# First mixing stage: attention's outputs wait in the place of its queries, and keys and values are projected early

## The chip, the cores and the metric

The kernel runs on one core of one Trainium2 chip. The metric is the device time of one execution in microseconds (us); a version's time is the median of several executions. One execution of each version is also recorded by the hardware profiler, and every duration below comes from such a record.

## The reference, cut to what matters

The program is two blocks one after the other on 256 tokens of width 1024. The first block has two layers, and each layer works on 256 latent tokens and 256 context tokens. The change is in the mixing part of the layers, above all of layer 0, where both kinds of tokens get an output:

```
hl = rms_norm(xl, norm_mix) * (1.0 + sc1_l) + sh1_l        # latents; hc is the same for the context
aq_l, ak_l, av_l, mq_l, mk_l, mv_l, mo_l, mg_l, pp_l = jnp.split(hl @ w_in, IN_OFFSETS, -1)
att_l = block_attention(q_l, jnp.concatenate([k_l, k_c], 1), jnp.concatenate([v_l, v_c], 1))
hm_c, hm_l = bidir_mlstm(...)              # a gated recurrence in two directions, 4 heads
ml_l = mlstm_readout(hm_l, mo_l, ml_norm)
pool_l = pool_mix(pp_l, pool_w, pool_scale)
xl = xl + g1_l * (jnp.concatenate([att_l, ml_l, pool_l], -1) @ w_out)
...
if with_ctx_out:                           # layer 0 only
    att_c = block_attention(q_c, k_c, v_c)
    ml_c, pool_c = ...
    xc = xc + g1_c * (jnp.concatenate([att_c, ml_c, pool_c], -1) @ w_out)
```

The factors sc, sh and g of both layers come from a further product, `silu(c) @ w_ada + b_ada`, whose matrix has 1024 x 6144 elements in each layer. After the mixing comes a gated feed-forward part in each layer. The second block (feed-forward, a mixer with a scan, feed-forward) isn't touched by the change.

## The kernel before

Values are kept transposed: 128 features on the partitions, tokens along the free axis, the 256 context tokens first and the 256 latents behind them. Each float32 product with a large weight is made of three matmuls (`mm3`, lines 235 to 237): weight and input are each split into a high part in a faster format and a low rest, on ScalarE (line 228 for weights, 256 for inputs) and VectorE (229 and 257). A column of 128 outputs of such a product (`dense`) loads its weights by SyncE's queue (line 219, function `raw`) into one of four buffers `wr`, splits them into `wh` (3 buffers) and `wl` (2 buffers), and multiplies. In layer 0 a column of the projection `w_in` has 8 x 3 matmuls of 512 tokens.

The projection of layer 0 has 17 columns. Each has a name: `a0` to `a3` are attention's queries, `ak` and `av` its keys and values, `k0 k1 q0 q1 v0 v1 g o0 o1` belong to the recurrence (mLSTM), and `p0 p1` to pooling. Their order is the string `order` in `MIX[0]`. The first three are computed before the stage proper, together with the norm that feeds them.

The rest of the stage is written as Python generators, which issue instructions until they `yield`. `_mix` lets them take turns. In each round every generator takes as many steps as its number in `MIX` says:

```
def _mix(*gens):
    live = [(iter(g), n) for g, n in gens]
    while live:
        for item in list(live):
            for _ in range(item[1]):
                if next(item[0], item) is item:
```

- `projections` issues one column a step, and marks it as there in the set `got` when it takes the next step.
- `mlstm` takes 25 steps (one for the gates, and for each of four heads four score tiles and two directions) and then three for its outputs. Its gates go through a small DRAM buffer `Md` (lines 872 and 891) on the same queue as the weights.
- `attention` takes one step for the split of the keys and then ten for each of the four query columns `a{j}`: four tiles of 128 queries by one head for the latents and one for their product with the values, then the same for the context. A tile is: scores on TensorE (line 788), maximum on VectorE, exponential on ScalarE, scaling on GpSimd (798), transposes on TensorE (801), a copy on ScalarE (802). The product with the values is line 807, into the PSUM tile `p3`, of which there is one.
- `pool_mix` (`fill`) takes four steps. Each is a chain of five or seven operations on GpSimd (lines 823 to 831), a matmul (834) and a split.
- `late` is the second half of the output product: 8 columns with the weights of rows 512 to 1023 of `w_out`, and it starts when mLSTM and pooling have given all their outputs.
- `ada` computes the factors, 26 steps in this stage: 16 for layer 0 and 10 that layer 1 needs only later. A step loads two blocks of 512 KB of `w_ada` into the same buffers `wr` and multiplies from them directly (line 374, 16 recorded matmuls a step), then a copy (383), two transposes (386) and two small operations on VectorE (388, 389). All of it goes through the one PSUM tile `p2`, which mLSTM's products (939) and the transposes of the values (479) use as well.

A waiting generator (`after`) yields without issuing anything. The framework then lays down a fixed order of instructions for each engine, in which the earlier issued goes first where both can run, and adds the semaphores. So instructions of one round can stand among those of its neighbours, but the loads on SyncE's queue stand in the order in which the rounds issue them, apart from loads that wait for data.

The outputs of attention, mLSTM and pooling go into `mixh` and `mixl`. In layer 0 these take the memory of the normed input `xh` and `xl`, which all projections read. So `free` in layer 0 is `after(*order)`: nothing may be written there until all 17 columns have been issued. Attention meets this wait right behind its first product with the values:

```
yield from free()
self.split(mixh[:, j, q0:q0 + 256], mixl[:, j, q0:q0 + 256], po)
```

When the generators are done, `resid_norm` computes the first half of the output product from attention's outputs (weights rows 0 to 511 of `w_out`, 16 loads of 256 KB), first for the context and then for the latents, together with the norm of the feed-forward part.

Layer 1 uses the same functions with `MIX[1]`. It has outputs for the latents alone, its `mixh` and `mixl` have memory of their own, and so `free` waits for nothing there.

Of the kernel before, what the change touches and what calls it, by code (L numbers as in the profile page):

```python
# [10 lines left out]
AF = mybir.ActivationFunctionType  # L11
# [9 lines left out]
    "natural_log": (AF.Ln,),  # L21
}
NOSYNC = mybir.DependencyInfo(mybir.DependencyClass.NoSync, mybir.DependencyReason.SCHED_ONLY)
MIX = {0: {'order': 'k0 g q0 v1 v0 a2 k1 q1 av a1 a0 a3 ak o0 p0 o1 p1', 'ada_own': 16, 'ada_next': 10, 'proj': 2, 'ml': 5, 'att': 1, 'fill': 1, 'late': 3, 'ada': 1, 'split': 0, 'split2': 1}, 1: {'order': 'ak k0 g a0 v0 q0 a1 av k1 q1 v1 a2 a3 p0 o0 o1 p1', 'ada_own': 10, 'ada_next': 0, 'proj': 3, 'ml': 9, 'att': 2, 'fill': 1, 'late': 1, 'ada': 1}, 2: {'in': 4, 'att': 2, 'solve': 1, 'att2': 5, 'gate': 1, 'even': 1, 'odd': 1, 'fill': 9, 'early': 5}, 'ada_ffn': [0, 0], 'norm0': 2, 'norm1': 2}
NEG = -1.0e30
EPS = 1e-6
GN_EPS = 64e-5
# [96 lines left out]
# [7 lines that stand above are left out]
                    live.remove(item)  # L131
                    break
        yield
# [18 lines left out]
def _run(g):  # L152
    for _ in g:
        pass


class Builder:
# [281 lines left out]
    def layer(self, l, pre, beside, done):  # L439

        nc, a, tc = self.nc, self.a, self.tc
        x, mod = self.x, self.mod[l]
        both = l == 0
        T0 = 0 if both else 256
# [3 lines left out]
        with ExitStack() as es:  # L448
# [9 lines left out]
            ak = ap.tile([128, 512], F32, name="ak")  # L458
# [128 lines left out]
            def projections():  # L587
                for i, p in enumerate(order[n0:], n0):
                    c, every, use = proj[p]
                    yield from self.dense(w, (c,), full if every else part, use, T=512 if every else T,  # L590
                                          halves=l and i < 2)
                    got.add(p)
                    if both and i == n0:
                        self.late_consts()
# [8 lines left out]
            mix = lambda k, c0, c1: (mixh[:, k, c0 - T0:c1 - T0], mixl[:, k, c0 - T0:c1 - T0])  # L603
            with tc.tile_pool(name=f"ml{l}", bufs=1, reuse_waits="tile") as mp:
                ml = _chain(self.mlstm(l, mp, gz, mq, mk, mvt, mo, mixh, mixl, T0, after, free), mark("ml"))
                att = self.attention(l, mp, aq, rq, nq, ak, avt, mixh, mixl, T0, after, free)
                fill = _chain(after("p0", "p1"), free(), self.pool_mix(l, pp, mixh, mixl, T0), mark("pool"))
                late = _chain(after("ml", "pool"), self.resid(a["w_out"][l], mix, ((4, 8),), T0, 512, m(2, 1), m(2, 0)))
                ada = _chain(self.ada(l, n["ada_own"], at=(2,)), self.ada(1, n["ada_next"], at=(2,)))
                _run(_mix((projections(), n["proj"]), (ml, n["ml"]), (att, n["att"]), (fill, n["fill"]),  # L610
                          (late, n["late"]), (ada, n["ada"])))
            if both:
                xn = self.room("xn", [128, 2, 8, 512], F32R)
# [139 lines left out]
        nc.gpsimd.tensor_mul(lat, lat, c1["cos"])  # L753
        nc.vector.tensor_add(lat, lat, rs)

    def attention(self, l, ap, aq, rq, nq, ak, avt, mixh, mixl, T0, after, free):
        nc = self.nc
        yield from after("ak")

        kk = ap.tile([128, 2, 2, 512], F32R, name="kk")  # L760
        half = lambda e: slice(64 * e, 64 * e + 64)
        for kv in range(2):
            for e in range(2):
                nc.scalar.activation(kk[half(e), kv, 0], ak[half(kv)], AF.Copy)
            for e in range(2):
                nc.vector.tensor_sub(kk[half(e), kv, 1], ak[half(kv)], kk[half(kv), kv, 0].bitcast(F32))
        yield
        streams = [(256 - T0, 4)] + ([(0, 2)] if T0 == 0 else [])
        for j in range(4):
            yield from after(f"a{j}")  # L770
            for q0, nk in streams:
                kv = j // 2
                qq = ap.tile([128, 2, 256], F32R, name="qq", bufs=2)
                for e in range(2):
                    src = aq[half(e), j, q0:q0 + 256]
                    nc.scalar.activation(qq[half(e), e], src, AF.Copy)
                    nc.vector.tensor_sub(qq[half(1 - e), e], src, qq[half(e), e].bitcast(F32))
                po = self.ps(3, [128, 256])
                pts = []
                for e in range(2):  # L780
                    pt = ap.tile([128, 4, 256], F32, name="pt", bufs=2)
                    pts.append(pt)
                    for qt in range(2):
                        ps = self.ps(1, [128, 512])
                        s = ps[:, 0:128 * nk]
                        c = (q0 + 128 * qt) // 128
                        for i in range(2):
                            nc.tensor.matmul(s, qq[:, e, 128 * qt:128 * qt + 128], kk[:, kv, i, 0:128 * nk],  # L788
                                             start=i == 0, stop=i == 1)
                        st = ap.tile([128, 4], F32, name="st", bufs=8)  # L790
                        nc.vector.reduce_max(st[:, 0:1], s, axis=AX.X)
                        nc.vector.tensor_mul(st[:, 1:2], st[:, 0:1], nq[:, c, 2 * j + e:2 * j + e + 1])
                        pr = ap.tile([128, 512], F32, name="pr", bufs=2)
                        p = pr[:, 0:128 * nk]
                        self.fn(p, s, AF.Exp, bias=st[:, 1:2], scale=rq[:, c, 2 * j + e:2 * j + e + 1],
                                accum_out=st[:, 2:3])
                        nc.vector.reciprocal(st[:, 3:4], st[:, 2:3])
                        nc.gpsimd.tensor_scalar(p, p, st[:, 3:4], 0.0, op0=OP.mult, op1=OP.add)
                        pp = self.ps(0, [128, 4, 128])
                        for kt in range(nk):  # L800
                            nc.tensor.transpose(pp[:, kt, :], p[:, 128 * kt:128 * kt + 128], self.ident)
                        nc.scalar.activation(pt[:, 0:nk, 128 * qt:128 * qt + 128], pp[:, 0:nk, :], AF.Copy)
                        yield
                yield from after("av")
                for kt in range(nk):
                    for e in range(2):
                        nc.tensor.matmul(po[64 * e:64 * e + 64, :], avt[:, kt, 64 * kv:64 * kv + 64], pts[e][:, kt, :],  # L807
                                         start=kt == 0, stop=kt == nk - 1)
                yield from free()
                self.split(mixh[:, j, q0:q0 + 256], mixl[:, j, q0:q0 + 256], po)  # L810
                yield

    def pool_mix(self, l, pp, mixh, mixl, T0):
        nc, c1 = self.nc, self.c1
# [841 lines left out]
```

## Time and profile before

| what | value |
|---|---|
| time of the runs shown | 1891.31 us median of 3 (1889.07 to 1895.42) |
| profiled execution | 1892.11 us, of which the recorded span is 1890.3 us |
| granted TensorE clock over the span | 0.985 of full speed |
| layer 0's mixing stage, from its fourth column to the last product of attention | 54.8 to 294.5 us of the span |
| first matmul of `resid_norm` behind it | 298.41 us |

The span runs from the first to the last recorded instruction; 1.8 us of the profiled execution lie around it. "Busy" of an engine is the time in which at least one of its instructions was running. Ends of matmuls are modelled, and a matmul overlaps with the next, so short pauses between small matmuls don't show as idle time. PEld is the loading of TensorE's weights, which overlaps with its matmuls.

### The profile page before, as it was taken

The numbers are of one execution on the slowest core, as the hardware profiler recorded it, in microseconds if no ns is written. First come the engines' busy times: TensorE is split into PE (matmuls) and PEld (weight loads), VectorE is DVE, ScalarE is ACT, GpSimd is POOL, SyncE is SP. The second block draws the span as 40 slices with busy tenths as digits, with TensorE's granted clock in tenths as the row PEclk, the third lists the DMA queues.
The fourth block names the chain that finished last, engine by engine and source line by source line (L and its number), as shares of the span: only waits on it lengthen the run. The fifth ranks groups of instructions, "written<-read, shape, count | busy, mean of one in ns | idle before, by whom it ended". The sixth has DMA issues, their size and how long they took to land.

```text
span 1890.3 us, 34101 instructions
## 1 busy us (share of the span) xinstructions
PE 1821.8 (96%) x13552; PEld 1602.4 (85%) x13552; DVE 1115.2 (59%) x2130; ACT 920.4 (49%) x1662; POOL 260.6 (14%) x357
## 2 busy tenths in 40 slices
PE   7999999999999999999999999998999999899998
PEld 4677567888888897878999999998989987799998
DVE  5566656433333365886676565568778854466554
ACT  4544467322222355666555544446755543354443
POOL 1011423000000021232000110023654010010000
PEclk8998999999999999999999999999999999999999
DMA  9443667332333365445667666665544430166664
GB/s 309 125 117 90 188 203 232 114 101 73 106 101 89 93 184 155 124 146 179 181 185 203 191 172 181 187 190 163 158 126 131 123 101 7 34 177 180 180 183 129
DMA packets 490607, 279.26 MB, mean 148 GB/s; under 512 B 18240, under 2 KB 487240, under 8 KB 490320
## 3 DMA queue, kind: packets, MB, share of 16 engines
q1 hardware_dynamic: 490016, 275.33, 50.0%
q8 instruction: 106, 1.74, 0.4%
q10 hardware_dynamic: 432, 1.75, 0.3%
q14 instruction: 53, 0.43, 0.1%
HBM read 274.93 MB, written 2.12 MB: 147 GB/s over the span
## 4 chain that ended last, share of the span: by engine, by line
PE 84%; DVE 6%; DMA 4%; issue 3%; ACT 2%; POOL 1%; SPq 0%; POOLq 0%; ACTq 0%; DVEq 0%
PE pd L235 17%; PE pd L237 17%; PE pd L236 17%; PE p L235 6%; PE p L236 6%; PE p L237 6%; PE p L374 2%; DMA wr<-in_w_in_dram 1%; DVE wl L229 1%; PE p L807 1%; PE p L788 1%; ACT wh L228 1%; PE p L1496 1%; DMA wr<-in_w_ada_dram 1%; DMA wr<-in_w_out_dram 1%
## 5 line engine op out<-in xcount | busy, mean ns | idle before, releaser
L228 ACT ACTIVATE wh<-wr 128x1024 fp32r<-128x1024 f32 (+4 forms) x450 | 436.9, 972 | 621.2 <-PE pd L236 297.5
L229 DVE TENSOR_TENSOR wl<-wr,wh 128x1024 fp32r<-128x1024 f32 (+4 forms) x450 | 510.4, 1135 | 181.6 <-PE pd L237 102.6
L235 PE MATMUL pd<-xh,wh 128*128 128x256 f32 (+1 forms) x1168 | 362.7, 312 | 13.7 <-ACT wh L228 7.8
L237 PE MATMUL pd<-xh,wl 128*128 128x256 f32 (+1 forms) x1168 | 357.7, 307 | 1.6 <-DVE wl L229 1.4
L235 PEld LDWEIGHTS pd<-xh,wh 128*128 128x128 f32 x1168 | 224.5, 193 | 32.1 <-ACT wh L228 9.3
L237 PEld LDWEIGHTS pd<-xh,wl 128*128 128x128 f32 x1168 | 224.6, 192 | 15.7 <-DVE wl L229 6.0
L235 PE MATMUL pd<-hh,wh 128*128 128x256 f32 (+1 forms) x781 | 228.2, 294 | 0.0
L236 PE MATMUL pd<-hl,wh 128*128 128x256 f32 (+1 forms) x781 | 227.3, 293 | 0.0
L236 PE MATMUL pd<-xh,wh 128*128 128x256 f32 x792 | 225.8, 285 | 0.0
L237 PE MATMUL pd<-hh,wl 128*128 128x256 f32 (+1 forms) x781 | 223.5, 294 | 0.2 <-DVE wl L229 0.2
L314 POOL TENSOR_TENSOR ssa<-ssa,sq 128x256 f32<-128x256 f32 x54 | 47.6, 882 | 805.0 <-ACT sq L312 536.2
L236 PEld LDWEIGHTS pd<-xh,wh 128*128 128x128 f32 x792 | 152.3, 192 | 1.9 <-issue 1.3
L235 PEld LDWEIGHTS pd<-hh,wh 128*128 128x128 f32 x781 | 146.8, 188 | 4.7
L236 PEld LDWEIGHTS pd<-hl,wh 128*128 128x128 f32 x781 | 146.7, 188 | 4.6
L237 PEld LDWEIGHTS pd<-hh,wl 128*128 128x128 f32 x781 | 144.8, 188 | 4.9 <-DVE wl L229 0.4
L236 PE MATMUL pd<-xl,wh 128*128 128x512 f32 (+1 forms) x376 | 132.1, 353 | 0.2 <-DVE xl L359 0.2
L732 DVE TENSOR_TENSOR sg<-sg,p 128x256 f32<-128x256 f32 (+1 forms) x66 | 33.6, 510 | 158.3 <-PE p L237 158.0
L235 PE MATMUL p<-xh,wh 128*128 128x256 f32 (+1 forms) x360 | 103.1, 286 | 0.0
L237 PE MATMUL p<-xh,wl 128*128 128x256 f32 x352 | 99.8, 283 | 0.0
L236 PE MATMUL p<-xh,wh 128*128 128x256 f32 x352 | 99.8, 283 | 0.0
L236 PEld LDWEIGHTS pd<-xl,wh 128*128 128x128 f32 x376 | 72.7, 194 | 11.1 <-DVE xl L359 1.5
L686 DVE SCALAR_TENSOR_TENSOR x<-pd,mod,x 128x256 f32<-128x256 f32 x88 | 40.8, 480 | 67.4 <-PE pd L237 67.4
(475 smaller groups left out, 3914.5 us busy)
## 6 DMA issues: line engine op xcount, KB each, us to landing
wr<-in_w_ada_dram SPq DMA_DIRECT2D x96, 512.0 KB, 4.6
wr<-in_w_in_dram SPq DMA_DIRECT2D x92, 512.0 KB, 3.8
wr<-in_w_ffn_gate_dram SPq DMA_DIRECT2D x44, 512.0 KB, 3.7
wr<-in_w_ffn_up_dram SPq DMA_DIRECT2D x44, 512.0 KB, 3.7
wr<-in_ffn_w_gate_dram SPq DMA_DIRECT2D x44, 512.0 KB, 3.7
wr<-in_ffn_w_up_dram SPq DMA_DIRECT2D x44, 512.0 KB, 3.8
wr<-in_ffn_w_down_dram SPq DMA_DIRECT2D x32, 448.0 KB, 3.5
wr<-in_w_out_dram SPq DMA_DIRECT2D x40, 256.0 KB, 3.1
```

What stands on the lines that cost most here:

```text
L228: nc.scalar.activation(h[:, :n], t[:, :n], AF.Copy)
L229: nc.vector.tensor_sub(l[:, :n], t[:, :n], h[:, :n].bitcast(F32))
L235: mm(ps, wh, xh, start=start, stop=False)
L236: mm(ps, wh, xl, start=False, stop=False)
L237: mm(ps, wl, xh, start=False, stop=stop)
L314: eng.tensor_add(acc, acc, sq)
L374: nc.tensor.matmul(bank[32 * g:32 * g + 32, 0:256], self.cs[:, k0 + g, :], v[:, g, :], start=k0 == 0, stop=k0 == 4)
L686: nc.vector.scalar_tensor_tensor(x[:, n, s:s + 256], ps[:, s - c0:s - c0 + 256], g(n), x[:, n, s:s + 256], op0=OP.mult, op1=OP.add)
L732: nc.vector.tensor_mul(g, g, ps)
L788: nc.tensor.matmul(s, qq[:, e, 128 * qt:128 * qt + 128], kk[:, kv, i, 0:128 * nk], start=i == 0, stop=i == 1)
L807: nc.tensor.matmul(po[64 * e:64 * e + 64, :], avt[:, kt, 64 * kv:64 * kv + 64], pts[e][:, kt, :], start=kt == 0, stop=kt == nk - 1)
L1496: mm(pg[e][rows(p), hf, i, :], src[rows(e), j, t], R.AR[rows(e), j, :, t], start=True, stop=True)
```

## The change

Four things are changed in the mixing stage.

1. In layer 0 attention's output is no longer split into `mixh` and `mixl` right away. It is copied from PSUM into the part of `aq` that held the queries of this column and these tokens, which have been used by then. So attention no longer waits for `free`. A new generator `attention_out` waits for `free`, and then splits each of the four columns of `aq` as a whole. `attention` marks a column as there with `got.add`. In layer 1 the split stays where it was.
2. The order of layer 0's columns: `ak`, `a0`, `av` and `a1` come as columns 5 to 8 where they were at 13, 11, 9 and 10; `a2` and `a3` come behind `v1`. The four columns at the end stay the same four.
3. The numbers of steps in a round of layer 0: `proj` 2 to 1, `ml` 5 to 3, `att` 1 to 4, `late` 3 to 2; the new generator takes 1, `ada` stays at 1.
4. In both layers two columns are issued before the first round.

```
-MIX = {0: {'order': 'k0 g q0 v1 v0 a2 k1 q1 av a1 a0 a3 ak o0 p0 o1 p1', 'ada_own': 16, 'ada_next': 10, 'proj': 2, 'ml': 5, 'att': 1, 'fill': 1, 'late': 3, 'ada': 1, ...
+MIX = {0: {'order': 'k0 g q0 v0 ak a0 av a1 k1 q1 v1 a2 a3 o0 p0 o1 p1', 'ada_own': 16, 'ada_next': 10, 'proj': 1, 'ml': 3, 'att': 4, 'fill': 1, 'late': 2, 'ada': 1, ...
...
-                att = self.attention(l, mp, aq, rq, nq, ak, avt, mixh, mixl, T0, after, free)
+                att = self.attention(l, mp, aq, rq, nq, ak, avt, mixh, mixl, T0, after, got)
+                out = self.attention_out(aq, mixh, mixl, after, free) if both else iter(())
...
-                _run(_mix((projections(), n["proj"]), (ml, n["ml"]), (att, n["att"]), (fill, n["fill"]),
+                dense = projections()
+                for _ in range(2):
+                    next(dense)
+                _run(_mix((dense, n["proj"]), (ml, n["ml"]), (att, n["att"]), (out, 1), (fill, n["fill"]),
                           (late, n["late"]), (ada, n["ada"])))
...
-                yield from free()
-                self.split(mixh[:, j, q0:q0 + 256], mixl[:, j, q0:q0 + 256], po)
+                if T0:
+                    self.split(mixh[:, j, q0:q0 + 256], mixl[:, j, q0:q0 + 256], po)
+                else:
+                    nc.scalar.activation(aq[:, j, q0:q0 + 256], po, AF.Copy)
                 yield
+            got.add(f"att{j}")
+
+    def attention_out(self, aq, mixh, mixl, after, free):
+
+        yield from free()
+        for j in range(4):
+            yield from after(f"att{j}")
+            self.split(mixh[:, j], mixl[:, j], aq[:, j])
+            yield
```

## Rows read from the trace of the kernel before

**Rows 1.** The page: busy time, share of the span and instructions of TensorE.
```profile
PE 1821.8 (96%) x13552; PEld 1602.4 (85%) x13552; DVE 1115.2 (59%) x2130; ACT 920.4 (49%) x1662; POOL 260.6 (14%) x357
```

**Rows 2.** Windows: stretch, length, busy by engine (instructions), granted clock, DMA share, GB/s.
```profile
0.00:50.00 50.00, 39.41 (x240) 22.33 (x240) 26.27 (x69) 21.55 (x39) 5.93 (x9) 0.90 0.95 309
54.80:190.00 135.20, 125.97 (x678) 99.17 (x679) 84.04 (x202) 67.59 (x141) 14.75 (x16) 0.96 0.38 110
190.00:250.00 60.00, 56.72 (x357) 35.55 (x355) 35.04 (x100) 26.36 (x62) 22.68 (x30) 0.97 0.56 176
250.00:294.50 44.50, 42.95 (x385) 24.86 (x384) 23.25 (x99) 32.69 (x86) 11.56 (x21) 1.00 0.78 249
54.80:294.50 239.70, 225.64 (x1416) 159.57 (x1416) 142.32 (x399) 126.64 (x288) 48.99 (x66) 0.97 0.50 152
350.00:400.00 50.00, 50.00 (x216) 40.24 (x215) 16.51 (x18) 14.81 (x19) 0.00 (x0) 1.00 0.36 104
```

**Rows 3.** Waits of TensorE, 54.8 to 190 us: total us, times, longest.
```profile
PE pd L235 <- ACT wh L228: 4.5, 2, 2.8
```

**Rows 4.** Waits of SyncE's queue, 60 to 190 us: total us, times, longest.
```profile
SPq L219 <- PE p L374: 45.5, 5, 18.0
...
SPq L872 <- DVE nt L863: 9.2, 1, 9.2
```

**Rows 5.** Timeline of SyncE's queue from 150 us: start, length, loads merged.
```profile
166.81 0.99 SPq L219 DMA_DIRECT2D wr<-in_w_in_dram  x2
174.39 31.35 SPq L219 DMA_DIRECT2D wr<-in_w_ada_dram  x10
...
233.29 58.63 SPq L219 DMA_DIRECT2D wr<-in_w_ada_dram  x26
294.32 21.65 SPq L219 DMA_DIRECT2D wr<-in_w_out_dram  x16
```

**Rows 6.** Groups of TensorE's instructions, 54 to 296 us: busy us, mean ns.
```profile
L374 PE MATMUL p<-wr,cs 128*32 128x256 f32 x400 | 29.7, 395 | 1.4 <-DVE mod L388 0.8 <-ACT nd L942 0.5
...
L788 PE MATMUL p<-kk,qq 128*128 128x512 f32 (+1 forms) x64 | 18.7, 382 | 0.7 <-ACT pr L202 0.7
L807 PE MATMUL p<-pt,avt 128*64 128x256 f32 x96 | 17.2, 392 | 1.0 <-ACT pt L802 0.9
L801 PE MATMUL p<-cm,pr 128*128 128x128 f32 x96 | 15.8, 278 | 0.0
L386 PE MATMUL p<-cm,ade 128*128 128x128 f32 x50 | 10.0, 282 | 1.8 <-ACT ade L383 1.8
...
L967 PE MATMUL p<-cm,hc 128*128 128x128 f32 x8 | 2.7, 333 | 1.5 <-DVE hc L966 1.5
```

**Rows 7.** Timeline of TensorE, the last projection's end.
```profile
192.98 0.40 PE L237 MATMUL pd<-xh,wl 128*128 128x512 f32 x1
```

**Rows 8.** Timeline of GpSimd: pooling's first and last operation, 24 in all.
```profile
169.54 0.64 POOL L823 TENSOR_TENSOR nt<-pp 128x271 f32<-128x271 f32 x1 [12.15 <-ACT pp L522]
...
217.70 0.73 POOL L831 TENSOR_TENSOR nt<-nt,pp 128x256 f32<-128x256 f32 x1
```

**Rows 9.** Timeline of TensorE, the change to the next part.
```profile
296.99 0.64 PE L374 MATMUL p<-wr,cs 128*32 128x256 f32 x8 [0.20 <-DMA wr<-in_w_ada_dram]
298.41 0.39 PE L235 MATMUL pd<-xh,wh 128*128 128x256 f32 x1 [0.78 <-ACT wh L228]
```

**Rows 10.** Groups of ScalarE, 54 to 300 us, that split attention's and mLSTM's outputs.
```profile
L256 ACT ACTIVATE xh<-p 128x256 fp32r<-128x256 f32 x8 | 3.0, 381 | 3.2 <-PE p L807 3.2
...
L256 ACT ACTIVATE xh<-mo 128x512 fp32r<-128x512 f32 x2 | 1.3, 630 | 0.9 <-DVE mo L968 0.9
```

**Rows 11.** The same on VectorE.
```profile
L257 DVE TENSOR_TENSOR xl<-p,xh 128x256 fp32r<-128x256 f32 x8 | 3.4, 420 | 5.6 <-ACT xh L256 5.6
...
L257 DVE TENSOR_TENSOR xl<-mo,xh 128x512 fp32r<-128x512 f32 x2 | 1.4, 693 | 0.6 <-ACT xh L256 0.6
```

**Rows 12.** Window: the slowest clock inside the stage (columns as in rows 2).
```profile
170.00:180.00 10.00, 7.21 (x32) 6.31 (x31) 5.30 (x15) 4.02 (x7) 4.02 (x7) 0.73 0.53 162
```

More of the change, by code (lines that the diff above doesn't have):

```diff
@@ L23 @@
 NOSYNC = mybir.DependencyInfo(mybir.DependencyClass.NoSync, mybir.DependencyReason.SCHED_ONLY)
-MIX = {0: {'order': 'k0 g q0 v1 v0 a2 k1 q1 av a1 a0 a3 ak o0 p0 o1 p1', 'ada_own': 16, 'ada_next': 10, 'proj': 2, 'ml': 5, 'att': 1, 'fill': 1, 'late': 3, 'ada': 1, 'split': 0, 'split2': 1}, 1: {'order': 'ak k0 g a0 v0 q0 a1 av k1 q1 v1 a2 a3 p0 o0 o1 p1', 'ada_own': 10, 'ada_next': 0, 'proj': 3, 'ml': 9, 'att': 2, 'fill': 1, 'late': 1, 'ada': 1}, 2: {'in': 4, 'att': 2, 'solve': 1, 'att2': 5, 'gate': 1, 'even': 1, 'odd': 1, 'fill': 9, 'early': 5}, 'ada_ffn': [0, 0], 'norm0': 2, 'norm1': 2}
+MIX = {0: {'order': 'k0 g q0 v0 ak a0 av a1 k1 q1 v1 a2 a3 o0 p0 o1 p1', 'ada_own': 16, 'ada_next': 10, 'proj': 1, 'ml': 3, 'att': 4, 'fill': 1, 'late': 2, 'ada': 1, 'split': 0, 'split2': 1}, 1: {'order': 'ak k0 g a0 v0 q0 a1 av k1 q1 v1 a2 a3 p0 o0 o1 p1', 'ada_own': 10, 'ada_next': 0, 'proj': 3, 'ml': 9, 'att': 2, 'fill': 1, 'late': 1, 'ada': 1}, 2: {'in': 4, 'att': 2, 'solve': 1, 'att2': 5, 'gate': 1, 'even': 1, 'odd': 1, 'fill': 9, 'early': 5}, 'ada_ffn': [0, 0], 'norm0': 2, 'norm1': 2}
 NEG = -1.0e30
@@ L754, in rope, with attention @@
         nc.vector.tensor_add(lat, lat, rs)
-    def attention(self, l, ap, aq, rq, nq, ak, avt, mixh, mixl, T0, after, free):
+    def attention(self, l, ap, aq, rq, nq, ak, avt, mixh, mixl, T0, after, got):
         nc = self.nc
```

## The prediction

> **What bounds the kernel now.** The page's first part comes first: TensorE is busy 96% of the span [rows 1], so the change can only give back what TensorE loses in the mixing stage. The windows by stretch say how much that is [rows 2]. From 54.8 to 294.5 us TensorE is busy for 225.6 of 239.7 us. The 14.1 idle us lie 9.2 in the projections (to 190), 3.3 in the output columns (to 250) and 1.6 in attention's end (to 294.5). Between 294.5 and the next part's first matmul at 298.4 [rows 9] another 2 us pass idle, since there only the last two steps of `ada` run (an estimate: 3.9 us less their matmuls at about 1 us a step). That makes 16 us of 243.6. The granted clock averages 0.96 and 0.97 before 250 [rows 2], which costs (1 - 0.96) x 135.2 + (1 - 0.97) x 60 = 7 us more; its worst ten microseconds, 0.73, hold the 2.8 us wait for a split weight [rows 3, 12].
>
> The waits tell why the projections lose time. TensorE waited 4.5 us in two pauses for ScalarE's split of a weight [rows 3]. Those weights were late because of SyncE's queue: it stood 45.5 us for slots that `ada`'s matmuls had yet to release, and 9.2 us for the gates that go through DRAM [rows 4]. It is one queue, so the weights stand behind both.
>
> Last, the queue's timeline shows what remains when the projections are over [rows 5]. The last two columns are loaded at 166.8, and 40 loads of `ada`, 20 steps, stand behind them (10 and 26 in the rows, four more among the output's). The final 26 took 58.6 us, 2.25 us each, while attention ran beside them; the DMA engines were 0.78 busy at 249 GB/s [rows 2]. So the end of this stage is nearly bound by transfers as well as by TensorE.
>
> **The change part by part.** *The rounds.* With one column a round, `p1` is issued in round 12 and `ada` has issued 11 steps by then. 15 steps, 30 loads, are left behind `p1`'s load in place of 40. Attention's 41 steps at 4 a round follow `a0` closely: columns 0 and 1 are issued in rounds 1 to 6, columns 2 and 3 in rounds 8 to 13. So nearly all of attention moves ahead of `p1`'s end. Its matmuls were 51.7 us of busy time, 32 tiles of 1.6 us [rows 6]. Pooling's four steps fall in rounds 13 to 16, the output columns in 17 to 20, and steps 21 to 26 of `ada` stand alone behind them: 12 loads where 26 stood.
>
> *The end of the stage* has two halves. From `p1`'s last matmul to the last pooling unit it was 193.4 to 218.4 [rows 7, 8], 25 us, with attention's scalings on GpSimd in between. The least is the 19 pooling operations that need `p1` or come after one that does, at about 0.7 us [rows 8], 13 us, and 2 to 3 for the matmul and split: I take 16, as attention is then nearly done. In these 16 us TensorE has six `ada` steps (29.7 + 10.0 us over 25 steps is 1.59 at most [rows 6]; some 1.25 without the overlap of the two groups, an estimate), about five late attention tiles and the outputs of mLSTM (2.7 us [rows 6]) and pooling (taken as the same): some 7.5 + 6.5 + 5 = 19 us, so it needn't idle. Then come the 8 output columns, 96 matmuls at 50 / 216 = 0.23 us [rows 2], 22.2 us, with nine `ada` steps, 11.3 us: 33.5 us of work. The loads for it, 18 of 512 KB and four late ones of 256 KB, are 10.5 MB: 42 us at 249 GB/s, or 34 at the 309 GB/s of the first 50 us [rows 2]. The middle, 38, leaves 4.5 us idle, and the change to the next part 1.4 [rows 9]. So the end idles 6 us (2 to 10) where 7 idled from 190 on. That is 1 us gained: the transfers that were hidden under attention are fewer, but stand alone.
>
> *The projections with attention inside.* What made TensorE idle for 9.2 us stays: the gates' way through DRAM, the slots, the shared `p2`. New is other work for these pauses: attention's tiles need neither `wr` nor `p2`. But each engine's order is fixed beforehand, so only a tile that stands ahead of the waiting matmul helps. Bounds: all 9.2 us filled, or none and the 5 us of idle time that lie beside attention from 190 to 294.5 added [rows 2]. I take a third filled, 3 us gained. ScalarE and VectorE are no bound: over the stage they are busy 126.6 and 142.3 of 239.7 us [rows 2].
>
> *The clock* followed the pauses. All 7 us come back if they all go, none if they all stay or move; I take 3.
>
> *Waiting in `aq`.* ScalarE copies eight tiles out of PSUM (0.38 us each, as the split's high part did [rows 10]), and later splits four of 512 tokens from memory (0.63 on ScalarE, 0.69 on VectorE, as for mLSTM's output [rows 10, 11]). Against the eight splits that fall away (3.0 + 3.4 us) ScalarE gets 2.5 us more and VectorE 0.6 less. I count nothing: they lie beside pooling's chain and the output columns. Without that cover the last would cost 0.63 + 0.69 = 1.3 us. Copying into `aq` waits for no one new, as the same tile's queries were split before its scores. What matters more is that `p3` comes free after a 0.38 us copy. Before, the first product held it until all columns were issued, and the next columns' products queued behind it.
>
> *Two columns ahead in layer 1.* The same instructions, in a slightly different order, with five `ada` steps in place of four behind the last projection. That is between nothing and one step's two loads, 4.5 us [rows 5], lost, and as much gained if its weights come earlier; I take zero, and 2 us either way for the range.
>
> **The sum.** 1 + 3 + 3 = 7 us. The profiled execution took 1892.1 us, 1890.3 of span and 1.8 around it, so the changed kernel takes 1885. The median shown, 1891.3, lies 0.8 lower; I don't correct for it.
>
> **A reading by another measure.** Weight loads are busy for 159.6 of 239.7 us, 67%, where the feed-forward's steady stretch has 40.24 of 50, 80% [rows 2]. The Trainium skill, *Perfetto Trace Analysis*, section "Identifying the Most-Contended Engine", holds matmul busy time to be a poor measure and weight-load time a better one, because pipelined instructions don't show their cost in the trace. By it the sum would start from 159.6 / 0.80 = 199 us, 40 us of slack in place of 16. The share in rows 2 agrees that the stretches with attention are the loosest (0.59 and 0.56 of their time); it is kept as the first rival.
>
> **The rivals.**
> 1. *More comes back than idle time shows.* The mechanism: matmul ends are modelled, and small matmuls of attention that wait on one another's chains look busy. From 190 to 294.5 weight loads fill 60.4 of 104.5 us; at 80% they would need 75.5, which leaves 29 us in which dense matmuls could stand. If half of it is used the time is 1892 - 7 - 15 = 1870. Against it: smaller matmuls don't reach the steady stretch's share anyway.
> 2. *No gain.* The weight waits stay, and attention's chain (scores, maximum, exponential, scaling, transposes, copy) puts its own waits into TensorE's fixed order. Or the clock takes the gain: at the end, `ada`'s matmuls alone fill 1.25 of some 4 us a step, and if the clock fell to 1.2 GHz for a third of the 22.2 us of output columns, that costs 7 us. The time is 1891. The Trainium skill, *TensorE: Matmul & The Clock Gate*, section "Why this matters for your kernels", warns of just such bursts between waits for transfers. The 0.73 behind a 2.8 us wait [rows 3, 12] agrees.
> 3. *Slower, by SyncE's queue.* In every round two `ada` loads now stand ahead of one column's load, where they stood ahead of two. Their slots are freed only when `ada`'s matmuls get `p2`, which mLSTM's products share, and mLSTM now takes more rounds. About 5.5 steps fell into the projections before, with 45.5 us of standing [rows 4]; now 11 do. If the pauses grow with them, the 9.2 idle us and the 5 us of clock become twice as much: 14 us more, against 1 at the end, 1905. It decides from the point where the projections idle more than 16 us (9.2 and the 7 of my sum). For it: the 4.5 us of waits have this cause. Against it: a round now holds attention's work too, so a load has longer to come.
>
> **How the numbers follow.** 0.3%, 5.7 us, is about what a measurement of this kernel can tell from no change; the line is at 1885.6. The forecast's case has 0.45, of which 0.38 lies beyond that line, as each of its terms can be larger; rival 1 has 0.12, rival 2 0.23, rival 3 0.20. So faster 0.38 + 0.12 = 0.50, same 0.07 + 0.23 = 0.30, slower 0.20. The range reaches from rival 1 to a part of rival 3: 1871 to 1897, with about 0.1 beyond either end. The forecast's own range is 1879 to 1889: the end's 2 to 10 us, with a fill of none to two thirds.
>
> **What the profile would show.** Scores (line 788) between 75 and 230 us in place of 160 to 294; four loads of `ada`'s kind for every two columns' loads until `p1`'s; `p1`'s last matmul at 230 to 240 where it was 193; behind the last output load 12 `ada` loads at 1.7 to 2.0 us each; `resid_norm`'s first matmul near 291. The prediction is wrong if that matmul stays at 298 or beyond, and wrong in its reasons if it moves while the idle time of the projections doesn't shrink, or if layer 1's stage accounts for more than 2 us of the difference.

## The result, and the profile after

The changed kernel takes **1945.06 us** (median of 4 runs, 1940.88 to 1955.17), the kernel before 1893.37 (4 runs): a ratio of **1.0292 [1.0259, 1.0325]**. (Ratios here and below are those on record, with their 95% intervals; they need not equal the quotient of two medians, which is 1.0273 here.) 1885 was predicted, with 1871 to 1897 as its range: it is 3% slower in place of a little faster. The profiled execution took 1946.82 us with a span of 1945.0, 54.7 longer than before's.

Three places of the two traces say where that arises. `resid_norm`'s first matmul stood at 298.41 us [rows 9] and stands at 339.53, 41.1 later. The first matmul of the second product in layer 0's feed-forward (tile `hh`) moved from 454.6 to 496.8, 42.2 later, so that little is lost between. TensorE's first weight load for layer 1's feed-forward moved from 888.7 to 943.2, 54.5 later. So layer 0's stage loses 41 us, layer 1's mixing stage 12, and all else about 1.

TensorE's line of the page, to set beside [rows 1]:

```profile
PE 1847.9 (95%) x13552; PEld 1612.6 (83%) x13552; DVE 1114.8 (57%) x2126; ACT 922.8 (47%) x1666; POOL 264.2 (14%) x357
```

It has 26 us more busy time in as many instructions: part of the loss is the same matmuls at a lower clock. The windows of the stage after (stretch, length, busy by engine, granted clock, DMA share, GB/s) show where:

```profile
54.80:85.00 30.20, 29.68 (x135) 21.13 (x134) 9.86 (x12) 13.77 (x21) 0.91 (x1) 1.00 0.35 105
85.00:125.00 40.00, 24.36 (x108) 18.28 (x110) 30.65 (x72) 23.27 (x52) 7.50 (x8) 0.65 0.20 53
125.00:190.00 65.00, 61.02 (x378) 42.94 (x370) 33.75 (x105) 34.18 (x89) 8.71 (x14) 0.98 0.39 114
190.00:256.00 66.00, 59.79 (x360) 43.89 (x360) 35.74 (x118) 34.52 (x81) 14.80 (x20) 0.95 0.31 93
256.00:300.00 44.00, 37.59 (x259) 20.06 (x260) 21.27 (x61) 18.64 (x42) 20.29 (x25) 0.92 0.64 203
300.00:340.00 40.00, 31.84 (x213) 18.09 (x211) 11.67 (x37) 6.02 (x13) 0.00 (x0) 0.86 0.76 243
```

The second stretch stands out: 40 us in which TensorE ran 108 matmuls at a clock of 0.65. In the kernel before, the same stretch is

```profile
85.00:125.00 40.00, 35.82 (x200) 27.36 (x201) 27.04 (x68) 22.53 (x51) 2.30 (x2) 1.00 0.61 173
```

Busy time by clock is 24.36 x 0.65 = 15.8 us of full-speed work in place of 35.8: 20 us lost there (an estimate, as the clock is a mean over the stretch). The last stretch, 300 to 340, is the other loose one.

**The first loose stretch** in SyncE's queue after (start, length, loads merged):

```profile
78.15 0.37 SPq L219 DMA_DIRECT2D wr<-in_w_in_dram  x1
78.61 6.38 SPq L219 DMA_DIRECT2D wr<-in_w_ada_dram  x2
101.56 3.07 SPq L887 DMA_DIRECT2D Md<-nt  x2
105.82 8.18 SPq L906 DMA_DIRECT2D nm<-Md  x3
125.03 0.37 SPq L219 DMA_DIRECT2D wr<-in_w_in_dram  x1
```

Between 85 and 125 us no load of a weight is issued. The gates' write to DRAM (`Md`) comes at 101.56, and stood at 79.42 before. Its wait in the queue, to set beside the 9.2 us of [rows 4]:

```profile
SPq L219 <- PE p L374: 36.7, 7, 11.0
SPq L887 <- DVE nt L878: 16.6, 1, 16.6
```

Why the gates are late is in VectorE's timeline (L872 is their first operation on it; the same operation, L857 there, began at 70.04 us in the kernel before):

```profile
83.37 1.23 DVE L229 TENSOR_TENSOR wl<-wr,wh 128x1024 fp32r<-128x1024 f32 x1 [4.68 <-ACT wh L228]
...
85.23 0.93 DVE L758 TENSOR_TENSOR ak<-ak,sq 128x256 f32<-128x256 f32 x1 [0.23 <-POOL ak L757]
...
87.07 1.37 DVE L770 TENSOR_TENSOR kk<-ak,kk 64x512 fp32r<-64x512 f32 x2
...
88.56 0.67 DVE L872 SCALAR_TENSOR_TENSOR sq<-nt 64x512 f32<-64x512 f32 x1
```

and in ScalarE's, where the gates' exponential (L202 on `sq`) begins at 91.19:

```profile
86.20 2.57 ACT L768 ACTIVATE kk<-ak 64x512 fp32r<-64x512 f32 x4 [2.38 <-DVE ak L758]
...
89.42 1.74 ACT L780 ACTIVATE qq<-aq 64x256 fp32r<-64x256 f32 x4
91.19 0.63 ACT L202 ACTIVATE sq<-sq 64x512 f32<-64x512 f32 x1
```

In each engine's order the gates now stand behind other work. On VectorE it is the split of the next column's weight (L229), for which the engine sat idle 4.68 us, as that weight was loaded only at 78.15, and then the keys' rotation (L758) and split (L770). On ScalarE, where their exponential runs, it is the split of the keys (L768) and of the first queries (L780). The Trainium skill, *PSUM — Partial Sum Buffer*, section "Engine vs sequencer instructions", calls the queues of these two engines strict FIFO; that agrees, as ScalarE had written the gates' operand by 78.4 us (`nt` at L871, 0.57 us from 77.82), and L872 began at 88.56, behind all that.

**The second loose stretch** in the queue, to set beside [rows 5]:

```profile
253.24 0.37 SPq L219 DMA_DIRECT2D wr<-in_w_in_dram  x1
253.70 26.83 SPq L219 DMA_DIRECT2D wr<-in_w_ada_dram  x10
...
303.51 2.25 SPq L219 DMA_DIRECT2D wr<-in_w_out_dram  x2
306.31 26.68 SPq L219 DMA_DIRECT2D wr<-in_w_ada_dram  x14
```

The last projection is loaded at 253.24 (166.81 before), and 14 `ada` loads, seven steps, stand alone behind the last output column (303.51). TensorE then, to set beside [rows 9]:

```profile
334.14 1.94 PE L374 MATMUL p<-wr,cs 128*32 128x256 f32 x16 [0.34 <-DVE mod L388]
336.64 0.69 PE L386 MATMUL p<-cm,ade 128*128 128x128 f32 x2 [0.56 <-ACT ade L383]
337.67 1.93 PE L374 MATMUL p<-wr,cs 128*32 128x256 f32 x16 [0.33 <-DVE mod L388]
339.53 0.58 PE L235 MATMUL pd<-xh,wh 128*128 128x256 f32 x1
```

A step comes every 3.5 us, with its 16 matmuls in 1.93 us where they took 1.07 in the kernel before (L374 at 255.29 us). That is the lower of the clock's two levels, 1.2 GHz: the granted clock from 329 to 339.5 us is 0.50. In these rows TensorE waits for the copy (L383) and the reduction (L388) of its own step, not for a load.

**Layer 1**, SyncE's queue, after (first two lines) and before:

```profile
852.26 6.87 SPq L219 DMA_DIRECT2D wr<-in_w_in_dram  x3
861.74 27.67 SPq L219 DMA_DIRECT2D wr<-in_w_ada_dram  x6
...
829.55 8.69 SPq L219 DMA_DIRECT2D wr<-in_w_ada_dram  x4
```

Behind the last projections stand six `ada` loads that take 27.7 us. There were four before, in 8.7 us. mLSTM's last product of this layer comes at 886.2 us, where it was 833.7: 10 us later than the 42.2 that the layer starts late.

### The profile page after: what moved, and what is told of

Read it like the earlier page. It is cut to its first block, busy times and chain, and to the rows that moved or that the text cites. A ratio compares the mean times of both kernels' runs of the same rounds, so it can differ in the third digit from the quotient of the medians.

```text
span 1945.0 us, 34093 instructions
## 1 busy us (share of the span) xinstructions
PE 1847.9 (95%) x13552; PEld 1612.6 (83%) x13552; DVE 1114.8 (57%) x2126; ACT 922.8 (47%) x1666; POOL 264.2 (14%) x357
## 4 chain that ended last, share of the span: by engine, by line
PE 85%; DMA 5%; DVE 4%; ACT 3%; issue 2%; POOL 0%; SPq 0%; ACTq 0%; POOLq 0%; DVEq 0%
PE pd L235 18%; PE pd L237 18%; PE pd L236 17%; PE p L235 6%; PE p L236 6%; PE p L237 5%; PE p L374 2%; DMA wr<-in_w_in_dram 2%; DMA wr<-in_w_ada_dram 1%; PE p L954 1%; DVE wl L229 1%; DMA wr<-in_w_out_dram 1%; PE p L811 1%; ACT wh L228 1%; PE p L1511 1%
## 5 line engine op out<-in xcount | busy, mean ns | idle before, releaser
L229 DVE TENSOR_TENSOR wl<-wr,wh 128x1024 fp32r<-128x1024 f32 (+4 forms) x450 | 510.4, 1135 | 193.2 <-PE pd L237 99.5
```

What stands on the lines that cost most here:

```text
L229: nc.vector.tensor_sub(l[:, :n], t[:, :n], h[:, :n].bitcast(F32))
```

## The experiments

Four theories. **A**: the gates lose their place to attention's preparation. **B**: one column per round puts more `ada` loads ahead of each column, and the slots that they wait for delay the projections. **C**: two columns ahead in layer 1 leave its end without dense work. **D**: attention ends too early and no longer covers the last `ada` loads. Ratios are to the kernel before, measured on the same chip.

### Layer 1 as before (e1)

```diff
-                for _ in range(2):
+                for _ in range(2 if both else 0):
```

> The changed kernel, but with no columns issued ahead in layer 1 (layer 0 keeps its two). In the changed kernel the stretch from layer 0's feed-forward to layer 1's feed-forward is 12 us longer than before, though layer 1's numbers are the same. Theory C, that the two columns issued ahead cost this in layer 1: 1933 us, 12 less than 1945, and layer 0 as in the changed kernel (resid_norm's first matmul at about 339). Rival, that layer 1 suffers from what layer 0 leaves behind (clock, order of the last factors): no difference, 1945.

Measured: 1930.62 us, 1.0214 [1.0193, 1.0235]. 14 us come back, and the queue has its four `ada` loads in 8.70 us again. So the two columns ahead carry layer 1's loss, as C says. That it arises because dense work is missing at the end is read from the trace and isn't tested apart.

### The gates ahead of the keys (e2)

```diff
-                for _ in range(2):
-                    next(dense)
+                next(dense)
+                self.late_consts()
+                next(ml)
+                next(dense)
```

(In layer 0 alone; the later call of `late_consts` goes.)

> The changed kernel, but in layer 0 mLSTM's step for the gates is issued between the two columns ahead, so before the keys' column ak. Theory A, that the gates stand behind the keys' and attention's first work on ScalarE and VectorE, and the weights behind the gates' DRAM round trip on SyncE's queue: the write to Md comes at about 80 us instead of 102, TensorE does not starve from 93 to 122, and the time falls by 20 to 25 us to about 1922. Theory B, that the two loads of factors ahead of every column starve TensorE throughout: at most 5 us less, 1940 or more.

Measured: 1925.81 us, 1.0182 [1.0148, 1.0216]. `Md` is written at 81.5 us, `resid_norm` begins at 322.0. 19 us come back: A holds. From 85 to 125 us TensorE is busy 36.30 us at a clock of 0.87, which by the same estimate is 16 of the 20 us that were lost there. The queue still issues no weight from 90.0 to 115.8 us in this run, so it wasn't the empty queue by itself that cost the time. What is left in this trace is the end:

```profile
288.92 25.21 SPq L219 DMA_DIRECT2D wr<-in_w_ada_dram  x14
...
310.00:322.00 12.00, 8.29 (x59) 2.45 (x55) 1.20 (x8) 1.78 (x4) 0.00 (x0) 0.50 0.79 257
```

### The gates' transfers on another queue (e3)

```diff
-            nc.sync.dma_start(self.Md[...
+            (nc.sync if l else nc.gpsimd).dma_start(self.Md[...
```

(The same for `nm`.) A rival of A: the late gates hurt only by holding up SyncE's queue.

> The changed kernel, but layer 0's transfers to and from Md are issued by GpSimd and not by SyncE, so that weights need not wait behind them. If theory A is right and it is the standing of the queue that hurts: the next weights come at about 90 us instead of 125 and 15 to 20 us are saved, 1927. If it is the lateness of the gates themselves (mLSTM's work starts late, whatever the queue): 5 us or less saved, 1940. Theory B: no difference.

Measured: 1947.89 us, 1.0298 [1.0272, 1.0323]; `Md` at 101.8. Nothing is gained. The queue no longer waits for the gates, but for `ada`'s slots instead:

```profile
SPq L219 <- PE p L374: 73.0, 7, 41.3
```

The `ada` matmul that frees the next slot stands behind the late mLSTM in TensorE's order (L374 at 125.00 us, behind L954 from 115.71). So it is the gates' own lateness, not their place in the queue.

### Waiting in `aq` alone (e4)

The order and the numbers of the kernel before, `range(0)` for the columns ahead.

> Of the change only the waiting in aq is left: the order of columns and the numbers of steps are those of before, and no column is issued ahead in either layer. Theories A and C both put the whole loss on the order of issue, so they expect the time of before, 1892 within 6 us. If the copies into aq or the late split cost something themselves, or tie up a buffer, it is 1900 or more.

Measured: 1890.65 us, 1.000 [0.9976, 1.0023]. The copies and the later splits cost nothing that can be measured.

### The gates and layer 1 together (e5)

e1's edit with e2's.

> The changed kernel with both of the last edits: mLSTM's gates are issued ahead of ak in layer 0, and no column is issued ahead in layer 1. If the two losses are separate things in separate stages they add up: 1945 - 19 - 14 = 1912 us, within 4. If one feeds the other, clearly more than that, 1918 or above.

Measured: 1913.53 us, 1.0099 [1.0061, 1.0137]. The two losses add (31.5 us of 14 and 19). Some 20 us remain, in layer 0: `p1` is copied out at 245.4 (193.4 before), `resid_norm` begins at 316.4. (e2 has the same layer 0 and begins it at 322.0: two profiled executions can differ by that much.) The next experiments start from e5.

### Fewer factors in the stage (e6, and e7 on the kernel before)

```diff
-'ada_next': 10
+'ada_next': 4
-'ada_ffn': [0, 0]
+'ada_ffn': [3, 3]
```

> As the kernel with gates first and layer 1 as before, but 6 of the 10 steps of layer 1's factors are computed beside layer 0's feed-forward and not in the mixing stage. Theory D, that the end of layer 0's stage is the factors alone (22 us between the last output column and resid_norm with gates first, TensorE at half clock), which attention covered before: the 22 us shrink to some 4, and the feed-forward gets 6 steps of about 1.25 us of matmuls: 10 to 16 us less than its sibling, about 1899. Rival, that something else holds resid_norm back: no gain, and up to 8 us more for the feed-forward, 1915 to 1920.

> The kernel before, with the same 6 steps of factors moved to the feed-forward. Theory D says that attention covered the factors' transfers in the kernel before, so that moving them moves only their matmuls: 1890 within 5 us. If the end of the stage was bound by transfers in the kernel before too, 8 us or more are saved, 1882 or less.

Measured: e6 1903.10 us, 1.0064 [1.0039, 1.0089]: `resid_norm` begins 21 us earlier, at 295.6, of which the feed-forward gives back some 10. e7 1901.70 us, 1.0044 [1.001, 1.0079], where 1890 within 5 us was expected: the same six steps cost the kernel before some 10 us there and shorten its stage by 1 (297.34 for 298.41). The price in the feed-forward was missed, the stage came as D says: at the end of the stage these steps lie bare in the change, and were covered before.

### More and fewer factors per column (e8, e9)

e8: `'ada': 2`. e9: every other number doubled, so one `ada` step for two columns.

> As the kernel with gates first and layer 1 as before, but with two steps of the factors in every round, so four loads of factors ahead of every column's load. Theory B, that the columns' weights wait behind the factors' slots: the projections get 10 us or more longer (the last projection ends well after 252), the end gets 20 shorter: 1900 to 1905. If the slots do not matter the projections keep their length and the time falls by all of the end, to 1892 or less. If the slots are all that matters it rises over 1912.

> As the kernel with gates first and layer 1 as before, but every number of steps is doubled except that of the factors, so that again two columns share one step of factors (two loads), as in the kernel before. Theory B (a column waits behind the loads of factors ahead of it): the last projection, copied out at 245.4 us in the sibling, is there by 230, which is more than the 6 to 8 us of matmuls of the five or six steps of factors that are no longer ahead of it. Theory D (factors alone at the end): those steps come out at the end at some 3.6 us each, 18 to 20 us, so the time does not fall: 1910 to 1920. If B is wrong the last projection is at 237 or later.

Measured: e8 1916.93 us, 1.0144 [1.0069, 1.022], with `p1` out at 284.9; e9 1933.89 us, 1.0223 [1.0186, 1.0259], with `p1` out at 213.5. The projections follow the `ada` loads ahead of them as B says, 40 us later with twice as many and 32 earlier with half. But the total is lower with neither, and both were missed: B had 1900 to 1905 for e8, and e9 was expected at 1910 to 1920. In e8 no factors are left behind the output columns, and yet `resid_norm` begins at 328.0, later than e5's 316.4: the projections lost more than the end gained. e9's trace shows what came in return there:

```profile
267.27 62.50 SPq L219 DMA_DIRECT2D wr<-in_w_ada_dram  x34
...
300.00:340.00 40.00, 30.92 (x207) 12.71 (x208) 5.88 (x27) 5.86 (x14) 0.00 (x0) 0.51 0.86 275
```

34 loads stand alone, with TensorE at its lower level for nearly all of that window. So B is real, but it's an exchange: factors that aren't loaded among the columns are loaded behind them.

### Attention slower (e10)

```diff
-'att': 4
+'att': 1
```

> As the kernel with gates first and layer 1 as before, but attention takes one step in a round and not four, so that most of it is issued beside the last factors. Theory D (attention was the cover of the factors' transfers, and the change took it away): no stretch of factors alone before resid_norm, which starts at 300 or earlier in place of 316.4; the time falls by 15 us or more, to 1898 or less. If the projections with one step of factors a column are what costs most (theory B alone), the gain is less than 8 us.

Measured: 1900.24 us, 1.005 [1.0034, 1.0065]; `resid_norm` begins at 299.95. The last 14 loads take longer and lie beside attention:

```profile
260.79 32.25 SPq L219 DMA_DIRECT2D wr<-in_w_ada_dram  x14
```

13 us come back, where D had 15 or more. The projections come earlier too (`p1` out at 219.5), as attention's steps no longer crowd them, so the time alone doesn't tell D from B. The windows do. Here are those of the kernel before, of e5 and of e10, each cut at `p1`'s copy, near the first of the last long run of factor loads, and at `resid_norm`:

```profile
54.80:193.40 138.60, 129.37 (x704) 101.26 (x705) 84.41 (x203) 67.98 (x142) 17.65 (x17) 0.96 0.37 107
193.40:233.00 39.60, 36.32 (x251) 22.15 (x250) 26.77 (x78) 19.98 (x48) 18.66 (x27) 0.96 0.66 206
233.00:298.40 65.40, 61.98 (x482) 36.67 (x480) 31.57 (x123) 39.74 (x101) 12.68 (x22) 1.00 0.70 223
...
54.80:245.40 190.60, 176.48 (x1043) 129.64 (x1041) 113.00 (x320) 110.01 (x255) 36.98 (x46) 0.97 0.37 111
245.40:285.00 39.60, 33.28 (x225) 17.32 (x224) 20.25 (x50) 15.37 (x32) 14.73 (x20) 0.91 0.65 206
285.00:316.40 31.40, 24.74 (x179) 12.63 (x177) 7.81 (x28) 4.54 (x10) 0.00 (x0) 0.86 0.80 259
...
54.80:219.50 164.70, 147.80 (x873) 109.61 (x876) 97.76 (x256) 83.87 (x183) 24.26 (x26) 0.98 0.44 128
219.50:260.80 41.30, 38.59 (x272) 23.68 (x273) 25.34 (x67) 20.00 (x49) 17.91 (x26) 1.00 0.64 205
260.80:300.00 39.20, 36.71 (x291) 22.93 (x289) 19.26 (x75) 24.48 (x63) 8.03 (x14) 1.00 0.65 204
```

Idle time and clock loss together (length times one less the granted clock, an estimate) are, in us:

| run | to `p1`'s copy | output columns | to `resid_norm` |
|---|---|---|---|
| before | 14.8 | 4.9 | 3.4 |
| e5 | 19.8 | 9.9 | 11.1 |
| e10 | 20.2 | 2.7 | 2.5 |

All that e10 gives back lies behind the projections, as D says, and none in them. e2, with e5's layer 0, has 21.8, 6.1 and 14.2, so a single part is known to some 4 us, and the 5 us that the projections lose more than before in both are hardly clear of that.

### The numbers before with the new order (e11, e12)

```diff
-'proj': 1, 'ml': 3, 'att': 4, 'fill': 1, 'late': 2
+'proj': 2, 'ml': 5, 'att': 2, 'fill': 1, 'late': 3
```

e12 has `'att': 1`, all the numbers before.

> The new order of columns with gates first, layer 1 as before and outputs waiting in aq, but with the numbers of steps of the kernel before, only attention at 2 a round instead of 1. B and D together say that what is left of the loss lies in the numbers: factors at one step per two columns, and half of attention behind the last projection. They expect the time of before or a little less, 1880 to 1893. If the early keys and queries themselves cost (their work on ScalarE and VectorE ahead of mLSTM's), 1898 or more.

> The new order of columns, the gates ahead of the keys, layer 1 without columns ahead, waiting in aq, and exactly the numbers of the kernel before, attention's 1 a round among them (e11 had 2). If the factors' loss of cover is what was left of the loss (theory D), attention stands beside the last factors again: p1 is over by about 188 us as in e11, resid_norm's first matmul comes at 296 to 300 in place of 306.6, and the time is 1888 to 1894, a ratio within 0.3% of 1. If early keys and values cost something by themselves, the time stays at 1898 or above although that matmul comes by 300, or it stays at 304 or later. Under 1886 would say that the change's order has a gain that its numbers had hidden.

Measured: e11 1900.77 us, 1.005 [1.0026, 1.0074]; e12 1902.74 us, 1.005 [1.0028, 1.0071]. Both missed what D promised by about 8 us, and fell on the other side that had been named, 1898 or more. `p1` is over as early as before (187.2 and 191.8) and in e12 attention's scores lie beside the last factors to 293.9, yet `resid_norm` begins at 306.6 and 309.5. So D does not explain this rest. In e12's trace mLSTM is late (TensorE's products of line L955: durations, then the first and the last start):

```profile
L955 PE MATMUL p<-mvt,W x160: 217/275/477, 94.9 to 199.4; 128*128 128x65 f32 x160
```

The last product came at 186.5 before. The new order puts `ak`, `a0`, `av` and `a1` ahead of `k1`, `q1` and `v1`, which mLSTM's second half needs. Pooling is late with it, though `p1` isn't: in GpSimd's order its last units stand behind a wait for mLSTM's outputs, and its last operation begins at 230.5 (217.7 before). The output columns need both; the last is loaded at 240.4 in place of 230.2, and the factors wait behind it.

### Which of the two: columns ahead, or their order (e13, e14)

e13: order and numbers of the kernel before, two columns ahead and the gates between them. e14: e12 with

```diff
-k0 g q0 v0 ak a0 av a1 k1 q1 v1 a2 a3
+k0 g q0 v0 k1 q1 v1 ak a0 av a1 a2 a3
```

> Order and numbers of the kernel before, waiting in aq, layer 1 as before; in layer 0 the first two columns are issued ahead of the rounds, with the gates' loads and mLSTM's first step between them. If the columns ahead carry the loss of e11 and e12, 28 loads stand behind the last output column as there, and the time is 1897 to 1904. If the order carries it (mLSTM's second half late), the last mLSTM product stays near 187 us, resid_norm's first matmul comes at 296 to 302, one factor step or 4.5 us at most later than before, and the time is 1889 to 1895.

> As e12 (numbers of the kernel before, gates first, layer 1 as before), but k1, q1 and v1 stand ahead of ak, a0, av and a1. If mLSTM's late second half carries the loss of e12, its last product falls back from 199.4 to about 187 us, the last output column's load from 240.4 to about 231, resid_norm's first matmul from 309.5 to 297 to 302, and the time from 1902.7 to 1889 to 1896. If early keys and values cost something in another way, or the columns ahead do, the time stays within 3 us of 1902.7.

Measured: e13 1891.65 us, 0.9999 [0.9983, 1.0016]; e14 1893.35 us, 1.0011 [0.9995, 1.0026]. The order carries it: e14 differs from e12 in nothing else. In e14:

```profile
L955 PE MATMUL p<-mvt,W x160: 217/275/477, 94.7 to 184.8; 128*128 128x65 f32 x160
...
231.95 58.58 SPq L219 DMA_DIRECT2D wr<-in_w_ada_dram  x28
...
298.38 0.58 PE L235 MATMUL pd<-xh,wh 128*128 128x256 f32 x1
```

`resid_norm` is back at 298.4, and pooling's last operation at 214.5. That mLSTM's place is what counts in the order, rather than the later place of keys and values, is read from these rows. (e13's profiled run, 1895.84 us, has 303.1, past the 302 expected; its median has no loss.)

### The better order at the change's numbers (e15)

e5 with e14's order.

> As e5 (the change's own numbers, gates first, layer 1 as before), but k1, q1 and v1 stand ahead of ak, a0, av and a1. If the order matters as it did at the old numbers (e12 to e14, 11 us of resid_norm's first matmul), mLSTM's last product comes 10 to 20 us earlier than e5's 230.2, that matmul at 302 to 307 in place of 316.4, and the time is 1900 to 1906. If at these numbers the factors' loads set the pace of the columns whatever their order, p1's end stays near 245, the last 14 factor loads stay alone, and the time stays at 1909 or above.

Measured: 1909.51 us, 1.0087 [1.0054, 1.012]. mLSTM's last product comes 33 us earlier than in e5 (197.0 for 230.2), where 10 to 20 was expected, and it helps by no more than the intervals: `p1` is out at 236.9, the 14 factor loads stand alone behind the last output column as in e5, and attention's scores are over at 260.0.

```profile
284.49 25.85 SPq L219 DMA_DIRECT2D wr<-in_w_ada_dram  x14
...
300.00:316.00 16.00, 11.57 (x86) 3.48 (x90) 2.00 (x12) 1.54 (x4) 0.00 (x0) 0.59 0.95 311
```

(The profiled run is the longest of the seven, 1921.62 us.) At these numbers the bare factors set the end (D); at the numbers before, mLSTM's lateness does. No run has the better order with one step of attention a round and one column, so what B costs when both other losses are away stays open.

## Why the prediction was wrong

**What makes TensorE idle stays** failed most. "The gates' way through DRAM" was listed among the causes that stay, and a third of the 9.2 idle us was to be filled. That way became 22 us later, because `ak` and the first queries pass the gates on VectorE and ScalarE: 19 us by e2, where 3 us gained were summed. Of the moved work only the matmuls and loads were counted, not its rotation and splits and the weight split between them, which stand ahead of the gates on two engines. By the rows above TensorE idles 26 us from 54.8 to 256, where 9.2 less 3 were expected to `p1`'s end. "ScalarE and VectorE are no bound" by their busy time was true and beside the point: it was their order.

**The end of the stage** failed in its size and sign. The counts were right: 30 loads behind `p1`'s, and 14 of them alone, where 12 were written. From `p1`'s end to `resid_norm` 16 + 38 + 1.4 = 55 us were written, and 72.5 were measured in after (267.0 to 339.5) and 71 in e5. About half of the difference is pooling, taken at 16 us and measured at 24 (to 291.1): GpSimd stood 7.8 us for pooling's matmuls (L849), which TensorE's order has among mLSTM's outputs. The other half is the loads. The working took the mean of transfers and dense work for them ("The middle, 38"), as if loads at the end of the queue could lie beside columns that are over by then. They take 25 to 27 us in after, e2, e5 and e15, and the granted clock falls to 0.50 towards their end (329 to 339.5 us in after, 310 to 322 in e2, 303 to 316 in e15). Without the gates 18 us are lost to `resid_norm` in e5, of which the table has some 13 behind `p1`, and e10 wins these back by attention's cover. What the order costs can't be added to that: e12 to e14 gain 0.4%, e5 to e15 0.1%.

**The clock** was to give back 3 us and took some instead: in the stage, length less granted clock by stretch sums to some 28 us ((1 - 0.65) x 40 + (1 - 0.98) x 65 + (1 - 0.95) x 66 + (1 - 0.92) x 44 + (1 - 0.86) x 40), against 7 before. It isn't a cause beside the others: most of it falls in the two loose stretches (14 us from 85 to 125, 5.6 from 300 to 340) and adds to their price.

**Layer 1** was bounded at 2 us, or 4.5 with a step bare; it measured 14 (e1). One step more does stand behind its last projection (12 loads for 10), as counted. What wasn't counted is that the dense columns, which come earlier, are missing beside mLSTM, attention and factors at the end; that this is the cause is likely and not shown.

**Right** were `aq`'s cost of nothing (e4) and the price of rival 3's mechanism in kind: `ada` loads ahead of each column do delay the projections (e8, e9). `p1`'s end was expected at 230 to 240 and came at 267; 245 without the late gates. Rival 3's mark, projections that idle more than 16 us, was passed (26), but by the gates and not by `ada`'s slots: with the gates ahead 14.1 us are left (e5), and of rival 3's 14 us at most some 5 are seen. By its own signs the forecast failed in full: that matmul stood beyond 298, at 339.5, and layer 1 accounts for 12 us.

**And the gain itself?** e14 has its scores 37 us earlier than before (from 132 us on, where it was 169), with none of the losses, and equals the kernel before. Its windows:

```profile
54.80:125.00 70.20, 67.16 (x312) 51.02 (x311) 48.16 (x94) 42.04 (x82) 3.44 (x3) 0.93 0.42 121
125.00:190.00 65.00, 63.57 (x383) 52.57 (x385) 41.15 (x122) 31.29 (x74) 16.73 (x18) 0.97 0.27 82
190.00:250.00 60.00, 56.91 (x394) 35.77 (x394) 33.95 (x97) 26.45 (x65) 19.95 (x29) 1.00 0.60 190
250.00:300.00 50.00, 44.38 (x371) 23.61 (x364) 22.12 (x89) 31.21 (x80) 9.85 (x17) 0.91 0.78 256
```

They leave 13.2 us idle, where the same four of the kernel before left 16.0, and the clock takes (1 - 0.93) x 70.2 + (1 - 0.97) x 65 + (1 - 0.91) x 50 = 11 us, where it took 7. To 190 us the idle time falls from 9.2 to 4.5, a half where a third was summed; the last 50 us give 2 back, and the clock the rest. That agrees with rival 2, but it is one profiled execution of each, and the differences are small. Of the 29 us in which rival 1 saw room, e14 finds none. No kernel tried is faster than the one before.

## What to carry to other kernels

Work that moves forward passes others on every engine's fixed order, so list what stands behind each of its small steps (rotations, splits, table loads), above all the head of a chain that goes through DRAM. A stream of loads with a fixed total needs cover at its end: ask what dense or other work is left beside its last load, for moving that work earlier leaves the stream bare, at a low clock. Where two consumers share the order of production (here mLSTM's second half and attention), give the first places to the one whose result the end of the stage waits for (e12 to e14; at the change's numbers, where something else set the end, it gained nothing, e15).

The Trainium skill, *Perfetto Trace Analysis*, section "Optimization Strategy", says that a kernel whose most-contended engine changes "may be improved by interleaving those regimes". e10 against e5 agrees: attention laid beside the bare loads gave 13 us.

## What the hardware showed unexpectedly

TensorE falls to its lower level and stays there without long pauses. In e5 the 16 matmuls of a step took 1.07 us at 298.54 and 1.40 at 300.95, though no pause since 296 us was longer than 0.56. In after's last steps it idles twice in 3.5 us, 0.33 and 0.56 us at a time, and runs at 1.2 GHz throughout, 1.93 us for 16 matmuls. A bare step then takes about as long as its transfers (1 MB at 309 GB/s would be 3.4 us, an estimate). In e9 the DMA engines moved 321 GB/s from 285 to 300 us (clock 0.83), and 292 from 300 to 316 (clock 0.50), where TensorE waited only for its own copies and reductions, a step each 3.52 us; in e15's window it was 311. So transfers and TensorE's own chain are close to each other as the bound, and the low clock costs the loads some 9% there. And the queue's pace shifts with what it stands behind: 34 loads in 62.5 us alone (1.84 each, e9), 14 in 25.0 to 26.7 alone (1.8 to 1.9), and 14 in 32.3 beside attention (2.3, e10), about the 2.25 of [rows 5].
